# A two-block network on one core: bias tables made in steps, last down sums kept in SBUF, gate operands loaded a step earlier

## The chip, the cores and the metric

One core of one Trainium2 chip runs the whole program. The metric is device time in microseconds (us): 3697.61 is the median of three runs of the kernel before (3693.20, 3697.61 and 3698.63). All arithmetic is float32; a matrix product is made of three passes over operands split into a high part (fp32r) and a low rest.

## The reference

Two blocks run one after the other on 2048 positions of 1024 features. The change touches the feed-forward part of the first block, the two norms behind it and a table for the attention of the second.

```python
def first_block(x, ...):
    h = concatenate([meta, x])                    # 16 + 2048 positions
    ...                                           # state-space mixer, pooling mixer, two norms
    h = h + mixed @ w_out
    n2 = rmsnorm(h, norm2_g)
    ff = silu(n2 @ w_gate) * (n2 @ w_up)          # 1024 -> 2816
    h = h + ff @ w_down                           # 2816 -> 1024
    return rmsnorm(h, final_norm_g)[:, 16:]

def second_block(x, p, ...):
    h = layer_norm(x, ln_in_g, ln_in_b)
    ...                                           # w_in_2; band attention and gated linear attention
    bias = rel_table[:, rel_idx]                  # relative bias, rel_idx clipped to 257 entries a head
    ...
    h = layer_norm(r + gate * (p @ w_ple), ln_g, ln_b)
```

## The kernel before

Features lie on the 128 partitions and positions in the free dimension, so a tile is 128 features by 512 positions (256 KB), and there are eight such tiles (m, or k) by four blocks of positions (b). The program is traced line by line into one list. A planner then simulates that list with its own costs and writes out the order of every engine's queue: an instruction that is ready in the simulation may be put ahead of ones traced before it. On the chip each queue (PE, DVE, ACT, POOL, and SP, which issues all loads; ACT issues all stores) runs strictly in its written order and waits where an operand is late.

`phase_main` (L794) goes through these stages around the change. `mix_out` (L954) multiplies the mixed features by w_out, adds x, stores h1 and sums squares. `gu_half(half)` (L1073) makes the gate and up products for two blocks: 22 columns j, each of seven half-size products (a Strassen-like scheme with operands 1, 2, 6, 5, 7, 3, 4), 84 matmuls of 512 positions a column. Its right-hand operands, 56 tiles, come from `gu_in(half)` (L984): four steps k, each of which loads four h1 tiles, scales them and splits seven combinations. Its left-hand operands come from `gu_w(j)` (L1028), a generator of five steps: split of the gate weights; load of the up weights and a subtraction; s2 with the split tiles wth and wtl; wsh and wsl; the split of the up weights. `gu_prime` (L1067) starts it for column 0. `down(half)` (L1174) multiplies the hidden features (tile hin, loaded back from hid_d) by w_down for one block after the other (i = 0, 1), 22 steps of 24 matmuls, then adds h1, stores h3 and sums squares (sq) and g-weighted values (sz). `norm(b)` (L1227) is the final RMS norm and the input layer norm of block b: `total` (L780) sums over partitions with a ones-matmul, a first pass writes z back to h3 and sums its squares, a second pass writes h2. `proj_half(0, 0)` (L1345) is the first half of the w_in_2 product: 16 groups of 24 matmuls of 256 columns, then 16 groups of 24 of 512.

Background generators stand in a list, `bg`, and `bg_step` (L893) advances the first of them by one `yield`: `gu_in(0)` during mix_out, `gu_in(1)` during down(0), norm(0) and norm(1) during gu_half(1), norm(2) and norm(3) during proj_half(0, 0). `bias_table` (L1414) is called whole between gu_half(0) and down(0): for each of eight heads it loads 257 values a partition into a tile `e`, negates them, copies one of them 511 times and stores 768 values.

Tiles of one tag share a fixed number of places: `raw` has four, `nh`, `wru`, `hid`, `st2`, `sq` and `s` two, `ls` three, `wsh` and `wsl` one, `x` in the pool fp twenty. `slot` (L1147) gives out six places in a fixed turn, wru, wru, wsh, wsl, hid, hid, to hin (22 a block) and to the four h1 pairs of each block; the bias tile `e` has the tag wru too. A place is given in the order of the trace, and its next user waits for the last reader of the one before.

Of the kernel before, what the change touches and what calls it, by code (L numbers as in the profile page):

```python
# [6 lines left out]
F32 = mybir.dt.float32  # L7
# [3 lines left out]
ALU = mybir.AluOpType  # L11
# [3 lines left out]
KT = 8  # L15
# [12 lines left out]
NFF = 22  # L28
# [7 lines left out]
class Build:  # L36
# [757 lines left out]
    def phase_main(self):  # L794
# [4 lines left out]
        with ExitStack() as ctx:  # L799
# [11 lines left out]
            with tc.tile_pool(name="ffn", bufs=1) as self.fp:  # L811
                self.xr.append(self.fp)
                with tc.tile_pool(name="psf", bufs=8, space=PSUM) as self.ps:
                    self.ffn = True
                    self.w_next.append(self.get_w(0))
                    self.xm = {b: [None] * KT for b in range(4)}
                    for part in (1, 0):
                        ins = [self.mix_in(b, part) for b in (0, 1)]
                        self.bg = ins
                        self.run_bg()  # L820
                        if part:
                            start = self.mix_start()
                    self.bg = [self.mix_in(b, part) for b in (2, 3) for part in (1, 0)]
                    self.mix_out((0, 1), start)
                    self.run_bg()
                    self.bg = [self.gu_in(0)]
                    self.mix_out((2,), steps=(4,))
                    self.mix_out((3,), steps=(3,), last=True)
                    self.run_bg()
                    for half in range(2):  # L830
                        self.bg = [self.norm(0), self.norm(1)] if half else []
                        self.gu_half(half)
                        self.run_bg()
                        if half == 0:
                            self.bias_table()
                            self.bg = [self.gu_in(1)]
                        else:
                            self.bg = [self.proj_in_steps()]
                        self.down(half)
                        self.run_bg()  # L840
                    self.bg = [self.norm(2), self.norm(3)]
                    xs = self.xs1
                    self.proj_half(0, 0, xs)
                    self.run_bg()
                    self.ffn = False
                self.xr.pop()
# [137 lines left out]
    def gu_in(self, half):  # L984


        r = []
        for i in range(2):
            t = self.fp.tile([128, 512], F32, tag="ls", name="r2", bufs=3)
            self.load(t, self.r2_d[2 * half + i:2 * half + i + 1].to_broadcast([128, 512]))  # L990
            r.append(t)
        self.xg = {p: [] for p in (1, 2, 6, 5, 7, 3, 4)}
        g = self.vec["norm2_g"]
        for k in range(4):
            x = {p: self.xtile() for p in self.xg}
            four = []
            for kk, i in ((k, 0), (k, 1), (k + 4, 0), (k + 4, 1)):
                t0 = half * 1024 + i * 512
                f = self.tmp("raw", 4)
                self.load(f, self.h1_d[kk * 128:(kk + 1) * 128, t0:t0 + 512])  # L1000
                self.stt(f, f, g[:, kk:kk + 1], r[i], ALU.mult, ALU.mult)
                four.append(f)
            b11, b12, b21, b22 = four
            t1 = self.tmp("t", 2)
            self.tt(t1, b12, b11, ALU.subtract)
            self.halves(x[1], b11)
            self.halves(x[2], b21)
            self.tt(b11, b22, t1, ALU.subtract)
            self.halves(x[6], b11, self.pool)
            self.halves(x[5], t1)  # L1010
            self.tt(b12, b22, b12, ALU.subtract)
            self.halves(x[7], b12)
            self.halves(x[3], b22, self.pool)
            self.tt(b21, b21, b11, ALU.subtract)
            self.halves(x[4], b21)
            for p in x:
                self.xg[p].append(x[p])
            yield 1

    def gu_load(self, j, up):  # L1020
# [132 lines left out]
    def down_start(self, half):  # L1153

        self.order = []
        for b in (2 * half, 2 * half + 1):
            self.order += [(b, j, None) for j in range(NFF)] + [(b, None, q) for q in range(4)]
        self.got = []

    def fetch(self):  # L1160
        if self.order:
            b, j, q = self.order.pop(0)
            if q is None:
                x = self.slot([128, 2, 512], F32R, "hin")
                self.load(x.bitcast(F32), self.hid_d[b, j])
            else:
                x = self.slot([128, 2, 512], F32, "h1")
                self.load(x, self.pair(self.h1_d, b, q))
            self.got.append(x)
# [4 lines left out]
    def down(self, half):  # L1174


        gf = self.vec["final_norm_g"]
        self.fetch()
        self.stats = []
        for i in range(2):  # L1180
            b = 2 * half + i
            pss = []
            for j in range(NFF):
                x = self.got.pop(0)
                hi, lo = self.get_w()
                for m in range(KT):
                    if j == 0:
                        pss.append(self.ps.tile([128, 512], F32, tag="ps", name="dn", bufs=8))
                    self.mm3(pss[m], [hi[:, m]], [lo[:, m]], [x[:, 0]], [x[:, 1]], first=j == 0, last=j == NFF - 1)
                self.fetch()  # L1190
                if (j % 5 == 2) if half == 0 else i:
                    self.bg_step()
            if i and half == 0:
                self.gu_prime()
            if i:
                sq, sz = (self.fp.tile([128, 512], F32, tag="st2", name="st2", bufs=2) for _ in range(2))
            else:
                sq, sz = self.tmp("s", 2), self.tmp("s", 2)
            for q in range(4):
                x = self.got.pop(0)  # L1200
                for e in range(2):
                    m = 2 * q + e
                    self.stt(x[:, e], pss[m], 0.5, x[:, e], ALU.mult, ALU.add)
                    self.add_sq(sq, x[:, e], m == 0)
                    if m:
                        self.stt(sz, x[:, e], gf[:, m:m + 1], sz, ALU.mult, ALU.add)
                    else:
                        self.ts(sz, x[:, e], gf[:, 0:1], ALU.mult)
                self.store(self.pair(self.h3_d, b, q), x)
                self.fetch()  # L1210
            self.stats.append((sq, sz))
        if half == 0:
            for _ in self.gw_steps:
                pass
# [12 lines left out]
    def norm(self, b):  # L1227

        vec = self.vec
        gf = vec["final_norm_g"]  # L1230
        c = slice(b * 512, b * 512 + 512)
        sq, sz = self.stats[b % 2]

        def tiles(k):
            out = []
            for i in range(k, min(k + 2, KT)):
                t = self.fp.tile([128, 512], F32, tag="nh", name="nh", bufs=2)
                self.load(t, self.h3_d[i * 128:(i + 1) * 128, c])
                out.append((i, t))
            return out  # L1240

        mt = self.fp.tile([128, 512], F32, tag="ls", name="mt", bufs=3)
        self.ts(mt, self.total(sz), 1.0 / D, ALU.mult)
        r = self.rstd(self.tp, self.total(sq), 512, 1.0 / D, EPS, "ls", 3, self.fp)
        ts = tiles(0)
        yield 1
        sv = self.tmp("s", 2)
        for k in range(0, KT, 2):
            for i, z in ts:
                self.stt(z, z, gf[:, i:i + 1], mt, ALU.mult, ALU.subtract)  # L1250
                self.add_sq(sv, z, i == 0)
                self.store(self.h3_d[i * 128:(i + 1) * 128, c], z)
            ts = tiles(k + 2)
            yield 1
        ts = tiles(0)
# [5 lines left out]
        s = self.rstd(self.tp, sr, 512, 1.0 / D, LN_EPS, "ls", 3, self.fp)  # L1261
# [152 lines left out]
    def bias_table(self):  # L1414


        for h in range(8):
            e = self.fp.tile([128, KT, 128], F32, tag="wru", name="e", bufs=2).rearrange("p a b -> p (a b)")
            self.load(e[:, 511:768], self.a["rel_rev"][:, h])
            self.ts(e[:, 511:768], e[:, 511:768], -1.0, ALU.mult)  # L1420
            self.dve.tensor_copy(out=e[:, 0:511], in_=e[:, 511:512].to_broadcast([128, 511]))
            self.store(self.eb_d[:, h * 768:(h + 1) * 768], e[:, 0:768])

    def att_setup(self):
        p = self.ap_
# [496 lines left out]
```

## Time and profile before

| what | value |
|---|---|
| median of three runs | 3697.61 us |
| the profiled execution, its own time | 3690.3 us |
| its span, first to last instruction | 3688.4 us |
| busy share: PE, PEld, DVE, ACT, POOL | 90, 75, 56, 42, 43 % |
| HBM read, written | 417.43, 154.33 MB |

PE is TensorE's matmul queue and PEld its weight loads; PEclk is the TensorE clock granted, 1.00 being 2.4 GHz and 0.50 being 1.2 GHz. "[6.60 <-ACT sq L54]" behind an instruction says that its engine stood idle for 6.60 us before it and that an ACT instruction that wrote tile sq ended the idle time. SPq and ACTq are the instructions that issue DMAs. The program's places of the change are found by the tile names: mo is mix_out, pa, pb and pc are gu_half, dn is down, pv and pt are proj_half, st is `total`.

### The profile page before, as it was taken

What the parts mean: (1) busy time and instruction counts of PE and PEld (TensorE: products, weight loads), DVE (VectorE), ACT (ScalarE), POOL (GpSimd) and SP (SyncE); (2) the same over time, 40 slices, a digit from 0 to 9 for tenths busy, and PEclk for the clock granted to TensorE, in tenths of its full rate; (3) what the DMA queues carried; (4) which work ended last, traced back from release to release, by engine and by line L of the source; (5) the groups of instructions that cost most, each with busy time, mean ns of one, the idle gap of its engine ahead of it and who ended that gap; (6) DMA issues with size and microseconds to landing.
All of it is one profiled execution on the core that took longest, in us unless ns stands there. A gap on an engine that the chain in (4) does not pass through costs nothing. (4 is left out here: it accounts for less than half of the span.)

```text
span 3688.4 us, 45750 instructions
## 1 busy us (share of the span) xinstructions
PE 3327.0 (90%) x16138; PEld 2757.7 (75%) x16138; DVE 2075.1 (56%) x3365; ACT 1564.6 (42%) x2748; POOL 1569.6 (43%) x1146
## 2 busy tenths in 40 slices
PE   7897798799996998999999966999999999989887
PEld 7676576588885886777887865798888987767666
DVE  7776555666667106777632052234666446788783
ACT  5344533334333213444432232234655445666553
POOL 1265544454444445555445432322322225354443
PEclk9998899899998999999999988999999999989998
DMA  9643375333226664444376556565665565555351
GB/s 254 132 127 88 109 214 174 109 115 112 105 103 228 205 222 155 155 143 148 109 238 235 185 175 188 167 179 171 175 174 147 167 172 173 162 146 154 118 174 38
DMA packets 338204, 584.87 MB, mean 159 GB/s; under 512 B 85772, under 2 KB 171300, under 8 KB 337976
## 3 DMA queue, kind: packets, MB, share of 16 engines
q1 hardware_dynamic: 231552, 427.60, 39.4%
q10 hardware_dynamic: 106424, 154.36, 12.0%
q8 instruction: 127, 2.08, 0.2%
q14 instruction: 101, 0.83, 0.1%
HBM read 417.43 MB, written 154.33 MB: 155 GB/s over the span
## 5 line engine op out<-in xcount | busy, mean ns | idle before, releaser
L44 POOL TENSOR_TENSOR wl<-wr,wh 128x1024 fp32r<-128x1024 f32 (+1 forms) x235 | 583.2, 2484 | 580.5 <-ACT wh L54 518.9
L54 ACT ACTIVATE wh<-wr 128x1024 fp32r<-128x1024 f32 (+2 forms) x289 | 301.4, 1046 | 468.2 <-PE dn L164 267.4
L163 PE MATMUL pt<-xh,wh 128*128 128x512 f32 x896 | 361.7, 404 | 14.7 <-ACT wh L54 7.6
L165 PE MATMUL pt<-xh,wl 128*128 128x512 f32 x896 | 359.2, 402 | 3.5 <-POOL wl L44 2.7
L164 PE MATMUL pt<-xl,wh 128*128 128x512 f32 x896 | 359.3, 401 | 0.2 <-DVE xl L44 0.2
L163 PE MATMUL dn<-hin,wh 128*128 128x512 f32 x704 | 278.9, 396 | 34.4 <-DMA hin<-hid_d 33.4
L164 PE MATMUL dn<-hin,wh 128*128 128x512 f32 x704 | 278.1, 395 | 0.0
L48 POOL TENSOR_SCALAR P<-P,rsm 128x640 f32<-128x640 f32 (+4 forms) x128 | 102.8, 804 | 343.6 <-DVE rsm L1497 286.3
L51 DVE SCALAR_TENSOR_TENSOR h<-dn,h 128x512 f32<-128x512 f32 x32 | 19.8, 680 | 368.4 <-PE dn L165 368.4
L1083 PE MATMUL pa<-xh,wh 128*128 128x512 f32 x528 | 211.4, 400 | 12.2 <-ACT xh L54 4.5
L165 PE MATMUL dn<-hin,wl 128*128 128x512 f32 x704 | 222.1, 396 | 0.4 <-POOL wl L44 0.4
L1083 PE MATMUL pa<-xl,wh 128*128 128x512 f32 x528 | 210.0, 398 | 2.3 <-DVE xl L44 2.3
L163 PEld LDWEIGHTS pt<-xh,wh 128*128 128x128 f32 x896 | 171.3, 191 | 51.9 <-ACT wh L54 9.9
L44 POOL TENSOR_TENSOR wl<-wru,wh 128x1024 fp32r<-128x1024 f32 x44 | 108.4, 2463 | 237.0 <-ACT wh L54 236.8
L1083 PE MATMUL pa<-xh,wl 128*128 128x512 f32 x528 | 206.8, 398 | 0.7 <-POOL wl L44 0.7
L165 PEld LDWEIGHTS pt<-xh,wl 128*128 128x128 f32 x896 | 170.4, 190 | 41.7 <-POOL wl L44 5.4
L164 PEld LDWEIGHTS pt<-xl,wh 128*128 128x128 f32 x896 | 171.0, 191 | 35.5 <-DVE xl L44 0.7
L44 POOL TENSOR_TENSOR hid<-raw,hid 128x512 fp32r<-128x512 f32 x88 | 127.0, 1453 | 164.9 <-issue 87.7
L163 PEld LDWEIGHTS dn<-hin,wh 128*128 128x128 f32 x704 | 132.9, 189 | 67.9 <-issue 33.9
L165 PEld LDWEIGHTS dn<-hin,wl 128*128 128x128 f32 x704 | 132.8, 189 | 31.8 <-POOL wl L44 0.8
L164 PEld LDWEIGHTS dn<-hin,wh 128*128 128x128 f32 x704 | 133.0, 189 | 30.8
L1360 PE MATMUL pv<-wh,xh 128*128 128x256 f32 (+1 forms) x512 | 148.0, 291 | 6.1 <-ACT wh L54 2.6
(463 smaller groups left out, 9280.6 us busy)
## 6 DMA issues: line engine op xcount, KB each, us to landing
hid_d<-hid ACTq DMA_DIRECT2D x88, 512.0 KB, 3.4
wr<-in_w_down SPq DMA_DIRECT2D x88, 512.0 KB, 3.5
hin<-hid_d SPq DMA_DIRECT2D x88, 512.0 KB, 4.3
wr<-in_w_out SPq DMA_DIRECT2D x56, 512.0 KB, 4.6
raw<-h_d SPq DMA_DIRECT2D x96, 256.0 KB, 4.0
wr<-in_w_in SPq DMA_DIRECT2D x44, 512.0 KB, 3.9
wru<-in_w_up SPq DMA_DIRECT2D x44, 512.0 KB, 3.6
wr<-in_w_gate SPq DMA_DIRECT2D x44, 512.0 KB, 3.4
```

The costliest lines, as they stand in the source:

```text
L44: return (eng or self.dve).tensor_tensor(out=o, in0=x, in1=y, op=op)
L48: (eng or self.dve).tensor_scalar(out=o, in0=x, scalar1=s1, scalar2=s2, op0=op0, **kw)
L51: return self.dve.scalar_tensor_tensor(out=o, in0=x, scalar=s, in1=y, op0=op0, op1=op1)
L54: return self.act.activation(out=o, in_=x, func=func, **kw)
L163: self.pe.matmul(ps, lhsT=hi[k], rhs=xh[k], start=(first and k == 0), stop=False)
L164: self.pe.matmul(ps, lhsT=hi[k], rhs=xl[k], start=False, stop=False)
L165: self.pe.matmul(ps, lhsT=lo[k], rhs=xh[k], start=False, stop=(last and k == n - 1))
L1083: self.pe.matmul(ps, lhsT=l_[:, k], rhs=x[k][r_], start=(first and k == n == 0), stop=(k == 3 and n == 2), skip_group_check=True)
L1360: self.pe.matmul(pt, lhsT=xh, rhs=whi[:, k % 4], start=(k == 0), stop=False)
```

## The change

`bias_table` becomes a generator that yields after each head, uses two tiles of the tag nh in place of one of the tag wru, stores in two parts, and runs as background of gu_half(0). `gu_in` takes its loads into tiles of the tags nh and s, issues those of step k + 1 at the end of step k, keeps r in st2 and t1 in ls, and has six yields in place of four; mix_out calls it at steps 4 and 6 of block 2 and 1 and 4 of block 3, down(0) at j = 1, 5, ... of its first block. `down(1)` writes its sums into tiles of its own (tag x of fp, eight a block) which `norm(2)` and `norm(3)` read and overwrite; the stores to h3 and the loads from it remain for norm(0) and norm(1) alone. norm(0) and norm(2) yield three times before they begin. At the end of down(0), `gu_w(0)` is advanced by two steps more before the sums, and the second block's h1 pairs skip the two wru places.

```diff
                     self.bg = [self.gu_in(0)]
-                    self.mix_out((2,), steps=(4,))
-                    self.mix_out((3,), steps=(3,), last=True)
+                    self.mix_out((2,), steps=(4, 6))
+                    self.mix_out((3,), steps=(1, 4), last=True)
                     self.run_bg()
                     for half in range(2):
-                        self.bg = [self.norm(0), self.norm(1)] if half else []
+                        self.bg = [self.norm(0), self.norm(1)] if half else [self.bias_table()]
                         self.gu_half(half)
                         self.run_bg()
                         if half == 0:
-                            self.bias_table()
                             self.bg = [self.gu_in(1)]
...
+        def fetch(k):
+            out = []
+            for n, (kk, i) in enumerate(((k, 0), (k, 1), (k + 4, 0), (k + 4, 1))):
+                t0 = half * 1024 + i * 512
+                f = self.tmp("s", 2) if n % 2 else self.fp.tile([128, 512], F32, tag="nh", name="nh", bufs=2)
+                self.load(f, self.h1_d[kk * 128:(kk + 1) * 128, t0:t0 + 512])
+                out.append((f, kk, i))
+            return out
+
+        four = fetch(0)
+        yield 1
         for k in range(4):
+            for f, kk, i in four:
+                self.stt(f, f, g[:, kk:kk + 1], r[i], ALU.mult, ALU.mult)
...
+            self.tt(t1, b12, b11, ALU.subtract)
+            self.tt(b12, b22, b12, ALU.subtract)
+            if k == 2:
+                yield 1
             x = {p: self.xtile() for p in self.xg}
...
+            if k < 3:
+                four = fetch(k + 1)
             yield 1
...
         for b in (2 * half, 2 * half + 1):
-            self.order += [(b, j, None) for j in range(NFF)] + [(b, None, q) for q in range(4)]
+            self.order += [(b, j, None) for j in range(NFF)]
+            if b == 1:
+                self.order.append(None)
+            self.order += [(b, None, q) for q in range(4)]
...
     def fetch(self):
+        if self.order and self.order[0] is None:
+            self.order.pop(0)
+            self.slot_n += 2
...
-                if (j % 5 == 2) if half == 0 else i:
+                if (j % 4 == 1 and not i) if half == 0 else i:
                     self.bg_step()
             if i and half == 0:
                 self.gu_prime()
+                next(self.gw_steps)
+                next(self.gw_steps)
...
-                    self.stt(x[:, e], pss[m], 0.5, x[:, e], ALU.mult, ALU.add)
-                    self.add_sq(sq, x[:, e], m == 0)
+                    o = x[:, e]
+                    if half:
+                        o = self.fp.tile([128, 512], F32, tag="x", name="h3", bufs=20)
+                        kept.append(o)
+                    self.stt(o, pss[m], 0.5, x[:, e], ALU.mult, ALU.add)
+                    self.add_sq(sq, o, m == 0)
...
-                self.store(self.pair(self.h3_d, b, q), x)
+                if not half:
+                    self.store(self.pair(self.h3_d, b, q), x)
...
+                if kept:
+                    out.append((i, kept[i]))
+                    continue
                 t = self.fp.tile([128, 512], F32, tag="nh", name="nh", bufs=2)
                 self.load(t, self.h3_d[i * 128:(i + 1) * 128, c])
...
+        for _ in range(3 if b % 2 == 0 else 0):
+            yield 1
         mt = self.fp.tile([128, 512], F32, tag="ls", name="mt", bufs=3)
...
-                self.store(self.h3_d[i * 128:(i + 1) * 128, c], z)
+                if not kept:
+                    self.store(self.h3_d[i * 128:(i + 1) * 128, c], z)
...
         for h in range(8):
-            e = self.fp.tile([128, KT, 128], F32, tag="wru", name="e", bufs=2).rearrange("p a b -> p (a b)")
-            self.load(e[:, 511:768], self.a["rel_rev"][:, h])
-            self.ts(e[:, 511:768], e[:, 511:768], -1.0, ALU.mult)
-            self.dve.tensor_copy(out=e[:, 0:511], in_=e[:, 511:512].to_broadcast([128, 511]))
-            self.store(self.eb_d[:, h * 768:(h + 1) * 768], e[:, 0:768])
+            e, f = (self.fp.tile([128, 512], F32, tag="nh", name="e", bufs=2) for _ in range(2))
+            self.load(e[:, 0:257], self.a["rel_rev"][:, h])
+            self.ts(e[:, 0:257], e[:, 0:257], -1.0, ALU.mult)
+            self.dve.tensor_copy(out=f, in_=e[:, 0:1].to_broadcast([128, 512]))
+            c = self.eb_d[:, h * 768:(h + 1) * 768]
+            self.store(c[:, 0:512], f)
+            self.store(c[:, 512:768], e[:, 1:257])
+            yield 1
```

## Rows read from the trace of the kernel before

**Rows 1.** PE by stretch: from:to, length, busy (matmuls), granted clock, DMA share, GB/s.

```profile
573.38:708.10 134.72, 101.67 (x372) 0.85 0.46 148
708.10:1128.20 420.10, 420.06 (x1814) 1.00 0.30 109
1128.20:1200.00 71.80, 40.42 (x160) 0.76 0.73 244
1405.00:1480.00 75.00, 56.72 (x231) 0.89 0.45 153
1480.00:1874.40 394.40, 386.97 (x1643) 0.99 0.41 141
2119.40:2328.50 209.10, 147.50 (x781) 0.85 0.55 177
2141.20:2156.00 14.80, 14.80 (x126) 1.00 0.57 182
```

**Rows 2.** PE's waits, whole run: who waited for whom, us, times, longest.

```profile
PE st L790 <- ACT sq L54: 59.4, 6, 31.5
PE dn L163 <- DMA hin<-hid_d: 33.4, 5, 30.7
...
PE pa L1083 <- ACT wth L54: 14.7, 1, 14.7
```

**Rows 3.** PE's waits between 573.38 and 708.10 us, the stretch around gu_in(0).

```profile
PE st L790 <- ACT sq L54: 9.9, 2, 6.6
PE pc L1083 <- ACT wsh L54: 6.6, 1, 6.6
PE pa L1083 <- ACT xh L54: 4.5, 1, 4.5
```

**Rows 4.** DVE's waits in the same stretch, the longest.

```profile
DVE raw L51 <- DMA raw<-h_d: 21.6, 8, 4.2
```

**Rows 5.** SP's queue at the beginning of down(0), order of time: start, length.

```profile
1124.95 4.66 SPq L57 DMA_DIRECT2D raw<-h_d  x3
...
1172.62 5.86 SPq L57 DMA_DIRECT2D e<-in_rel_rev  x2
...
1186.09 12.41 SPq L57 DMA_DIRECT2D hin<-hid_d  x2
```

**Rows 6.** The bias tile e: ns min/median/max, first and last start; then landing times.

```profile
L48 DVE TENSOR_SCALAR e<-e x8: 283/288/2495, 1138.8 to 1180.9; 128x257 f32<-128x257 f32 x8
L1421 DVE COPY e<-e x8: 414/427/2442, 1139.1 to 1182.9; 128x511 f32<-128x511 f32 x8
...
DMA to landing us min/median/max: 2.3/5.0/7.3
```

**Rows 7.** SP's queue between down(0) and gu_half(1), order of time.

```profile
1409.29 3.69 SPq L57 DMA_DIRECT2D wru<-in_w_up  x2
```

**Rows 8.** DVE between down(0) and gu_half(1), order of time, first and last sum.

```profile
1402.52 2.48 DVE L51 SCALAR_TENSOR_TENSOR h<-dn,h 128x512 f32<-128x512 f32 x4 [104.88 <-PE dn L165]
...
1419.19 2.82 DVE L51 SCALAR_TENSOR_TENSOR st<-h,v_final_norm_g,st 128x512 f32<-128x512 f32 x1
```

**Rows 9.** PE's waits between 2119.4 and 2328.8 us, proj_half(0, 0).

```profile
PE st L790 <- ACT sq L54: 49.1, 3, 31.5
PE pt L163 <- ACT wh L54: 5.7, 1, 5.7
PE pv L1361 <- POOL wl L44: 2.9, 1, 2.9
```

**Rows 10.** DVE's waits between 2135 and 2253 us, the longest.

```profile
DVE nh L51 <- DMA nh<-h_d: 43.1, 16, 6.5
```

**Rows 11.** DVE by line, 2119 to 2253 us: count, busy us, mean ns, idle before.

```profile
L51 DVE SCALAR_TENSOR_TENSOR nh<-nh,v_final_norm_g,mt 128x512 f32<-128x512 f32 x16 | 13.0, 819 | 31.3 <-DMA nh<-h_d 30.7 <-ACT ev L54 0.6
L51 DVE SCALAR_TENSOR_TENSOR st<-h,v_final_norm_g,st 128x512 f32<-128x512 f32 x7 | 10.6, 1520 | 0.2
```

**Rows 12.** POOL by line, 2135 to 2253 us, the squares of the norms summed.

```profile
L44 POOL TENSOR_TENSOR s<-s,sq 128x512 f32<-128x512 f32 x14 | 18.7, 1333 | 50.6 <-ACT sq L54 50.4
```

More of the change, by code (lines that the diff above doesn't have):

```diff
@@ L988, in gu_in @@
         for i in range(2):
-            t = self.fp.tile([128, 512], F32, tag="ls", name="r2", bufs=3)
+            t = self.fp.tile([128, 512], F32, tag="st2", name="r2", bufs=2)
             self.load(t, self.r2_d[2 * half + i:2 * half + i + 1].to_broadcast([128, 512]))
@@ L993, in gu_in @@
         g = self.vec["norm2_g"]
-        for k in range(4):
-            x = {p: self.xtile() for p in self.xg}
[L996 to L1005, printed above, removed]
+        def fetch(k):
[8 more added lines that the diff above has]
+        yield 1
+        for k in range(4):
+            for f, kk, i in four:
+                self.stt(f, f, g[:, kk:kk + 1], r[i], ALU.mult, ALU.mult)
+            b11, b12, b21, b22 = (f[0] for f in four)
+            t1 = self.fp.tile([128, 512], F32, tag="ls", name="t1", bufs=3)
+            self.tt(t1, b12, b11, ALU.subtract)
+            self.tt(b12, b22, b12, ALU.subtract)
+            if k == 2:
+                yield 1
+            x = {p: self.xtile() for p in self.xg}
             self.halves(x[1], b11)
@@ L1010, in gu_in @@
             self.halves(x[5], t1)
-            self.tt(b12, b22, b12, ALU.subtract)
             self.halves(x[7], b12)
@@ L1194, in down @@
                 self.gu_prime()
+                next(self.gw_steps)
+                next(self.gw_steps)
+            kept = []
             if i:
@@ L1202, in down @@
                     m = 2 * q + e
-                    self.stt(x[:, e], pss[m], 0.5, x[:, e], ALU.mult, ALU.add)
-                    self.add_sq(sq, x[:, e], m == 0)
+                    o = x[:, e]
[4 more added lines that the diff above has]
+                    self.add_sq(sq, o, m == 0)
                     if m:
-                        self.stt(sz, x[:, e], gf[:, m:m + 1], sz, ALU.mult, ALU.add)
+                        self.stt(sz, o, gf[:, m:m + 1], sz, ALU.mult, ALU.add)
                     else:
-                        self.ts(sz, x[:, e], gf[:, 0:1], ALU.mult)
-                self.store(self.pair(self.h3_d, b, q), x)
+                        self.ts(sz, o, gf[:, 0:1], ALU.mult)
+                if not half:
+                    self.store(self.pair(self.h3_d, b, q), x)
                 self.fetch()
-            self.stats.append((sq, sz))
+            self.stats.append((sq, sz, kept))
         if half == 0:
@@ L1231, in norm @@
         c = slice(b * 512, b * 512 + 512)
-        sq, sz = self.stats[b % 2]
+        sq, sz, kept = self.stats[b % 2]
         def tiles(k):
```

## The prediction

> **What bounds the kernel now.** I read the busy shares first: PE is busy 90% of the span, no other engine over 56%. So I went on to PE by stretch [rows 1], to see where the missing tenth lies. The gate product of the first half runs 1814 matmuls in 420.06 of 420.10 us at clock 1.00: that is the price of a matmul of 512 positions when nothing is late, 0.2316 us. Those of 256 columns cost 14.80/126 = 0.1175 us. With these, each stretch that the diff touches has a floor and an excess:
>
> - A, gu_in(0) around the end of mix_out: 372 x 0.2316 = 86.2, took 134.7, excess 48.6 us, of it 33.1 idle; the rest is matmuls at a clock below 1.00 after the stalls (0.85 in the mean), so an idle us costs 48.6/33.1 = 1.47 us here.
> - B, the beginning of down(0): 160 x 0.2316 = 37.1, took 71.8, excess 34.7, 31.4 idle.
> - C, the beginning of gu_half(1): 231 x 0.2316 = 53.5, took 75.0, excess 21.5, 18.3 idle.
> - D, proj_half(0, 0): 384 of 256 columns 45.1, the other 397 at 0.2316 91.9, together 137.0; took 209.1, excess 72.1, 61.6 idle.
>
> In all 176.9 us that edits of this kind can reach. PE's waits over the run say who holds them [rows 2]: totals of the norms waiting for a split sum 59.4, down waiting for hin 33.4, a gate product waiting for wth 14.7. They are three of the largest, and each lies in one of the four stretches.
>
> **The change part by part.** Durations are of the profiled execution, 3690.3 us (its span 3688.4); the median of the runs is 7.3 us above it, and I take the sum of gains from the median.
>
> *B, the bias table.* Down(0) stands still for one hin, 30.7 us. SP's order shows why: the last two loads of e go out at 1172.62, and the hin that PE needs only at 1186.09 [rows 5]. The tag decides it: e and hin share the two wru places, eight e were traced ahead of the seventh hin, so that hin waits for four rounds of load, two DVE operations and a store. With e in nh the six places of `slot` belong to hin alone. What stays are the sixteen 256 KB loads of gu_in(1), which have this place in both versions. Bounds: all 34.7 gone, or 15 if these loads alone keep SP's queue late by half. I take 30: each hin is then asked for up to six steps of 24 x 0.2316 = 5.6 us ahead.
>
> *The bias heads' new place.* Two yields in odd columns and one in even ones put the eight heads into the first six columns of gu_half(0), 84 x 0.2316 = 19.5 us each. They add 8 x (0.29 + 0.43) = 5.8 us of DVE, up to 8 x (2.50 + 2.44) = 39.5 where POOL is in the way, and eight loads, sixteen stores on ACT's queue; a load or a store takes 2.3 to 7.3 us to land [rows 6]. The cover is good (DMA share 0.30, PE never idle [rows 1]) but the queues are strict: an early-placed negation waits for its load and holds the DVE work behind it, a store waiting for the copy holds ACT. The least is nothing. The most I charge is the slower rival's price below. I take 2 us lost.
>
> *A, gu_in(0).* PE waits there 9.9 us for totals, 6.6 for wsh, 4.5 for xh [rows 3], and DVE waits eight times, 21.6 us, for h1 tiles [rows 4]: its scaling of an h1 tile stands in front of mix_out's evacuation and of the weight splits, and only four raw places, shared with mix_out's own x tiles, carry the loads. Afterwards four loads of a step go out together, a step ahead, from places of their own: one wait per k in place of two, so half of 21.6. Not covered: step 3's loads can only start when step 2's tiles are read, and those need the x places that block 3 of mix_out frees at its end, so one round (median 5.0 us to land, as for e in [rows 6]) and some 5 us of DVE stay behind the last mo, against 63 gate matmuls (14.6 us) that k = 0 to 2 already allow. I count the longer of the two total waits (6.6) and two thirds of wsh and xh (7.4) as gone: 14 us idle, times 1.47 = 21. Ends: nothing, if the planner writes the scaling as close behind the loads as now; 34 if only the first total (3.3), weight splits and their clock remain.
>
> *C, the gate operands.* The up weights for column 0 are asked for at 1409.29 [rows 7], after PE has left down, since their wru place held an h1 pair. s2 and wth then queue on DVE behind the sums of down, which fill it from 1402.5 to 1422.0 [rows 8], and PE waits 14.7 us [rows 2]. Afterwards the place is free from j = 17 on, four steps or 22 us earlier, and s2 and wth are traced ahead of the sums, in a stretch where DVE had been idle for 104.9 us [rows 8]. wsh and wsl come next: their places now hold the first two h1 pairs, and wsl's subtraction stays behind the sums, not before 1422. PE then has products 1, 2, 6 and two thirds of 5, 44 matmuls or 10.2 us from 1405.0: it waits for about 7 us instead of 14.7. Gain 8, and 1 for norm(0) coming three steps later: 9. Ends: 0 (POOL's splits are as late as wth was) and 15.
>
> *D, the sums kept.* DVE waits sixteen times, 43.1 us, for nh tiles coming back from h3 [rows 10], and PE's totals behind it 49.1 us, another 5.7 for a weight split that ACT could not reach behind the norm's operations [rows 9]. The change takes away 32 loads of 256 KB and the stores of h3 and z, 16 MB; the arithmetic stays. What is late next is arithmetic: a first pass is 8 scalings on DVE (0.82 us), 8 squares on ACT and 7 additions on POOL (1.33) [rows 11, 12], paced by POOL at 10 to 11 us. From norm(2)'s first total to its second lie six background steps, of 24 x 0.1175 = 2.8 us, 17 us, and norm(3)'s lie partly among the 512-column groups (5.6 us each), so both are covered. Three groups (8.5 us) now stand ahead of norm(2)'s first total. Left: 2.9 for a w_av split on POOL, about 5 around the first totals, while DVE and POOL work off down's sums, 2 at the end, 2 of clock: 12 of 72. Gain 60. Ends: 24 (ports, below) and 69.
>
> Here the Trainium skill speaks against the change: SBUF — State Buffer, section Who interferes with whom, says that a DVE instruction with two SBUF inputs and a GpSimd instruction that reads SBUF take one shared port in turn, each for its whole length. The trace bears it out: the same kind of operation takes 0.82 us in a first pass that waits for DMA and 1.52 beside POOL's back-to-back additions [rows 11]. By that rule a first pass without DMA pauses takes 8 x (0.82 + 1.33) = 17 us in place of 11.
>
> *Sum.* 30 - 2 + 21 + 9 + 60 = 118 us; 3697.6 - 118 = 3580. Everything after 2330 has the same instructions; but the planner orders anew, for which I allow 10 us either way.
>
> **The rivals.**
> - *Ports.* First passes take 8 x (0.82 + 1.33) = 17 to 18 us, and if the planner writes the totals directly behind each other, PE stands through two of them, 36 us: D gives 72 - 12 - 36 = 24, the sum is 82, 3616 us. For: [rows 11]. Against: six steps of other matmuls are traced between.
> - *The lead does nothing.* The planner already hoists whatever is ready, so moved yields and earlier `next` calls change nothing where a place or a queue is the limit: A gives 5, C 2, the sum is 95, 3603 us. For: the first loads of gu_in(1), traced at j = 2 of down(0), go out at 1124.95 already [rows 5], before down's own stretch begins. Against: the tags change too, not the order alone.
> - *All of it.* A 34, B 34, C 15, D 69, nothing lost: 152, 3546 us. Against: POOL's splits and the first totals stay.
> - *Slower: the bias heads break the gate stage.* nh has two places, one head fills both, and SP is strict: a load of e waiting for the store before it holds the gate and up weights queued behind it. Price: 8 heads x (one landing 5.0 + load 5.0 + 0.7 DVE) = 86 us, times 1.47 for the clock 126 us; more than the 118 gained, so 3706 us. It decides from 80 us idle, 10 us a head; below it the change still gains. Against: the weights are loaded a column of 19.5 us ahead, and one or two heads fall into a column.
>
> **How the numbers follow.** Forecast 50%, ports 18%, the lead does nothing 16%, all of it 12%, slower 4%. The forecast alone runs from 3560 to 3602 (A and D 10 us each way, B and C 5, the new order 10). The range goes to the ports' price plus the planner's 10 above, and to the full gain less 6 below: 3540 to 3628. All cases but the last lie below 3690, which is 0.2% under the median, about what a measurement of this kernel can tell from no change: faster 0.95, same 0.01, slower 0.04.
>
> **What would show it.** B: no wait of down for hin over 3 us, e loads between 700 and 830 us. D: no h3 loads after down(1), PE's waits for totals in proj_half(0, 0) under 10 us in all, its stretch near 149 us. A: DVE's waits for h1 tiles halved, the stretch to the steady gate columns near 114 us. C: the wait moved from wth to wsl or wl and halved. The gate stage still at clock 1.00 and within 2 us of 420. Wrong would be a wait for totals of over 20 us in D, PE idle in the first six gate columns, or a new wait after 2330.

## The result, and the profile after

The changed kernel takes 3607.5 us, the median of four runs (3604.7 to 3610.5); the kernel before took 3695.6 beside it. The ratio is 0.9761, 95% interval [0.9744, 0.9778]: 88 us faster, where 118 were forecast. That is inside the stated range, but 5.5 us above the 3560 to 3602 of the forecast alone. Run again beside the last three versions it gave 3605.0. The profiled executions differ by 85.7 us of span (3688.4 and 3602.7), and the points where PE changes stage divide that up (the first stretch begins where PE stops for the first total, at 573):

| stretch on PE | before | after | gain | forecast |
|---|---|---|---|---|
| last blocks of mix_out (gu_in(0) beside them) | 98.5 | 106.9 | -8.4 | |
| gu_half(0) | 456.5 | 449.9 | 6.6 | 19 with the row above (A 21, heads -2) |
| down(0) (B) | 276.7 | 256.2 | 20.5 | 30 |
| gu_half(1) (C) | 469.6 | 456.0 | 13.6 | 9 |
| down(1) | 244.9 | 243.8 | 1.1 | 0 |
| proj_half(0, 0) to the first score matmul (D) | 220.7 | 170.5 | 50.2 | 60 |
| everything behind | 1348.4 | 1346.1 | 2.3 | 0 |

PE by stretch, cut at these points, before and then after; the columns are those of [rows 1]:

```profile
573.38:671.90 98.52, 82.13 (x319) 0.90 0.53 169
671.90:1128.40 456.50, 439.81 (x1870) 0.98 0.30 108
1128.40:1405.05 276.65, 243.99 (x1040) 0.94 0.65 217
1405.05:1874.60 469.55, 443.84 (x1873) 0.97 0.42 143
2119.45:2340.10 220.65, 158.97 (x825) 0.85 0.56 179
```

```profile
573.20:680.10 106.90, 84.00 (x320) 0.87 0.54 168
680.10:1130.00 449.90, 438.66 (x1870) 0.99 0.34 120
1130.00:1386.20 256.20, 246.36 (x1038) 0.98 0.64 212
1386.20:1842.20 456.00, 442.29 (x1879) 0.99 0.42 145
2086.00:2256.50 170.50, 156.67 (x832) 0.95 0.45 149
```

PE's waits over the whole run after, the two longest in total (who waited for whom, us, times, longest):

```profile
PE z L753 <- ACT ge L54: 29.0, 9, 9.2
PE st L790 <- ACT sq L54: 19.7, 5, 8.2
```

Against [rows 2], down's wait for hin (33.4) and the gate product's for wth (14.7) are gone, and the totals' wait has fallen from 59.4 to 19.7. Of these 19.7, 13.5 lie in the first stretch, where 9.9 lay before [rows 3]:

```profile
PE st L790 <- ACT sq L54: 13.5, 2, 8.2
PE mo L165 <- DVE wl L44: 6.0, 2, 5.5
PE pa L1092 <- DVE wtl L44: 3.8, 1, 3.8
PE mo L165 <- POOL wl L44: 2.6, 1, 2.6
PE pa L1092 <- POOL wl L44: 2.1, 1, 2.1
```

This is the view (573.2 to 700 us) where the term with the largest miss, A, failed. In place of the waits of the first gate products, 6.6 for wsh and 4.5 for xh [rows 3], there are 3.8 for wtl and 2.1 for wl; but the totals' waits grew (6.6 to 8.2 and 3.3 to 5.3) and a weight split of mix_out became late. Next, DVE in that stretch (from:to, length, busy, clock, DMA share, GB/s); before, it was busy for 63.1 of the same 100 us:

```profile
600.00:700.00 100.00, 77.44 (x78) 0.86 0.50 153
```

What stands in front on DVE's queue can be read off in order of time:

```profile
614.81 0.75 DVE L51 SCALAR_TENSOR_TENSOR s<-s,v_norm_g,r 128x512 f32<-128x512 f32 x1 [2.00 <-DMA s<-h_d]
615.48 1.22 DVE L44 TENSOR_TENSOR wl<-wr,wh 128x1024 fp32r<-128x1024 f32 x1
...
635.77 2.65 DVE L51 SCALAR_TENSOR_TENSOR s<-s,v_norm_g,r 128x512 f32<-128x512 f32 x2 [1.66 <-DMA s<-h_d]
...
641.41 0.68 DVE L44 TENSOR_TENSOR t<-mo,raw 128x512 f32<-128x512 f32 x1
```

PE ran out of work at 611.3 and waited 5.5 us for the weight split of 615.48, whose other half was ready at 610.4; a scaling of gu_in that still waits for its load stands ahead of it. PE ended the last sum of block 2 at 635.5; its evacuation came at 641.41, behind seven operations of gu_in, and the total waited 8.2 us.

The bias heads run at the beginning of gu_half(0), but eight in 48 us, some three to a column, where one or two were expected. The tile e after (ns min/median/max, first and last start), and ACT's waits for it between 690 and 760 us:

```profile
L57 SPq DMA_DIRECT2D e<-in_rel_rev x8: 327/328/333, 694.4 to 738.7; - x8
L48 DVE TENSOR_SCALAR e<-e x8: 281/298/1378, 699.3 to 741.2; 128x257 f32<-128x257 f32 x8
...
  DMA e<-in_rel_rev: 10.3, 6
```

```profile
ACT wsh L54 <- DVE e L48: 8.1, 1, 8.1
ACT wsh L54 <- DVE e L1451: 7.0, 1, 7.0
ACT raw L54 <- DVE e L1451: 5.4, 1, 5.4
```

SP's queue, which issues the loads, waited in turn for the heads' stores (688 to 760 us):

```profile
SPq L57 <- DMA eb_d<-e: 35.7, 9, 5.9
```

One head's store on ACT waits for DVE's copy, the copy for DVE's negation, the negation for a load (10.3 us of DVE in six waits) that SP often could issue only after an earlier store had landed. As I read it, what stands behind the store on ACT, an evacuation or a weight split, is what PE lacks next. (A wait "for e" of the split wsh is a wait of the queue: the store, which is not shown as busy, stands ahead of it.)

In proj_half(0, 0) PE's waits came down from [rows 9] to these, 13.8 us in all:

```profile
PE st L790 <- ACT sq L54: 5.1, 2, 3.8
PE pt L163 <- DVE ev L51: 2.2, 1, 2.2
PE st L791 <- DVE sl L44: 2.0, 2, 1.7
PE pv L1390 <- ACT wh L54: 1.9, 1, 1.9
PE pt L165 <- POOL wl L44: 1.7, 1, 1.7
PE pv L1390 <- DVE ev L44: 0.9, 1, 0.9
```

### The profile page after: what moved, and what is told of

The parts are those of the page before. It is cut to its first block, busy times and chain, and to the rows that moved or that the text cites. A ratio compares the mean times of both kernels' runs of the same rounds, so it can differ in the third digit from the quotient of the medians.

```text
span 3602.7 us, 45654 instructions
## 1 busy us (share of the span) xinstructions
PE 3326.9 (92%) x16138; PEld 2761.8 (77%) x16138; DVE 2092.3 (58%) x3365; ACT 1565.5 (43%) x2750; POOL 1569.8 (44%) x1146
## 4 chain that ended last, share of the span: by engine, by line
PE 36%; DVE 7%; DMA 5%; ACT 3%; issue 2%; POOL 1%; SPq 0%; ACTq 0%; DVEq 0%; POOLq 0%
PE pt L165 4%; PE pt L163 4%; PE pt L164 4%; PE pa L1092 3%; PE dn L163 2%; PE dn L164 2%; PE dn L165 2%; PE pv L1562 2%; PE s L1520 1%; PE pv L1391 1%; PE pv L1392 1%; PE pc L1092 1%; PE pv L1390 1%; PE tp L1546 1%; DMA raw<-mix_d 1%
## 5 line engine op out<-in xcount | busy, mean ns | idle before, releaser
L1525 DVE CUSTOM_DVE_ANT_0 P<-s,bias 128x640 f32<-128x640 f32 (+4 forms) x128 | 94.5, 738 | 108.5 <-PE s L1520 59.9
```

The source lines that it names most:

```text
L1525: self.dve.tensor_tensor_reduce(out=v3(P[:, 0:w]), in0=sp[:, 0:np_, 0:n], in1=v3(bias[:, 640 - w:640]), scale=1.0, scalar=3e38, op0=ALU.ad ...
```

## Experiments

All stretches below are cut as in the table. In these runs the last one, with the same matmuls (6859 to 6867 records), took between 1334 and 1352 us without any order by kernel, and so the stretches tell more than the totals.

### 1. The bias table back in the wru places

```diff
-            e, f = (self.fp.tile([128, 512], F32, tag="nh", name="e", bufs=2) for _ in range(2))
+            e = self.fp.tile([128, KT, 128], F32, tag="wru", name="e", bufs=2)...
...
-                        self.bg = [...] if half else [self.bias_table()]
+                        self.bg = [...] if half else []
...
+                            self.bias_table()
                             self.bg = [self.gu_in(1)]
```

> The changed kernel with one part undone: the bias table is again one call between gu_half(0) and down(0), with its tile e in the tag wru. Theory (places): the eight tiles stand again between the sixth and the seventh hin, PE waits for hin 20 to 30 us and down(0) takes some 22 us longer, while the gate stage, rid of the heads, gives back 2 to 8; about 3622 us, 3617 to 3630. Rival (the queue): down(0) was held by gu_in(1)'s loads in SP's queue, which now have places of their own; then this kernel stays within 5 us of the changed one, 3602 to 3612, and no wait for hin exceeds 10 us.

3623.8 us, ratio 0.9816 [0.9797, 0.9834], 16 more than the change, as the theory has it. gu_half(0) and down(0), and the wait that came back:

```profile
678.30:1119.70 441.40, 434.79 (x1870) 0.99 0.32 112
1119.70:1400.50 280.80, 244.53 (x1038) 0.95 0.63 208
```

```profile
PE dn L163 <- DMA hin<-hid_d: 26.9, 3, 25.1
```

Down(0) pays 24.6 us for the shared places (280.8 against 256.2); gu_half(0) without heads is 8.5 us shorter (441.4 against 449.9). So the step is worth 16 net, and the heads cost four times the 2 us that I charged.

### 2. gu_in as before: loads in their own step

```diff
-                f = self.tmp("s", 2) if n % 2 else self.fp.tile(..., tag="nh", ...)
+                    f = self.tmp("raw", 4)
...
-                    self.mix_out((2,), steps=(4, 6))
-                    self.mix_out((3,), steps=(1, 4), last=True)
+                    self.mix_out((2,), steps=(4,))
+                    self.mix_out((3,), steps=(3,), last=True)
...
-                if (j % 4 == 1 and not i) if half == 0 else i:
+                if (j % 5 == 2) if half == 0 else i:
```

> The changed kernel with gu_in as it was (places raw, t and ls, no loads a step ahead, four yields at the old steps). Theory (the work only moved): in the changed kernel gu_in's DVE operations come earlier and stand in front of mix_out's evacuations and weight splits instead of the first gate column, so undoing it changes little: 3600 to 3614 us, and mix_out's last matmul falls back by some 8 us while the first gate columns lose the same. Rival (the gain is there but the bias heads eat it): undoing gu_in costs the 21 us that were forecast for it, 3622 to 3634 us.

3605.1 us, 0.9759 [0.9739, 0.9779]: no difference in the total. As a whole the new gu_in gains nothing in this pair of runs: what it gains in one place is given back in another. From its own profile, mix_out's end, gu_half(0) and down(0), each against the row of after above:

```profile
580.80:682.00 101.20, 85.59 (x319) 0.88 0.53 166
682.00:1136.20 454.20, 438.70 (x1869) 0.98 0.30 108
1136.20:1388.60 252.40, 243.85 (x1039) 0.99 0.66 223
```

The old gu_in is 5.7 us better beside mix_out and 3.8 better in down(0). But the heads stood elsewhere in this run, and only run 11 with runs 1, 5 and 10 separates the two (below).

### 3. The down sums stored again

```diff
-                    if half:
+                    if False:
                         o = self.fp.tile([128, 512], F32, tag="x", name="h3", bufs=20)
...
-                if not half:
+                if True:
                     self.store(self.pair(self.h3_d, b, q), x)
```

> The changed kernel with down(1) again writing its sums to h3 and norm(2) and norm(3) loading them back twice; the three yields before norm(2) stay. Theory (DMA paced the norms): proj_half(0, 0) takes some 50 us longer, 3650 to 3662 us, with DVE waiting for nh again for over 30 us. Rival (half of the gain came from norm(2) beginning three steps later): it takes 20 to 35 us longer, 3628 to 3643 us.

3647.7 us, 0.9878 [0.9860, 0.9896], 40 more than the change: between the two ranges, nearer to the theory's. DVE waits again for nh, 45.9 us in fifteen times. The stretch of proj_half(0, 0), and PE's and DVE's waits that came back:

```profile
2088.30:2297.90 209.60, 159.84 (x824) 0.86 0.60 188
```

```profile
PE st L790 <- ACT sq L54: 43.8, 3, 31.1
```

```profile
DVE nh L51 <- DMA nh<-h_d: 45.9, 15, 6.2
```

209.6 against 170.5: 39 us of D's 50 belong to the kept sums. The other 11 (220.7 to 209.6) come with the rest of the change: the first total waits 3.9 us in this run, as in the change, where it waited 8.5 before, and the 5.7 for wh [rows 9] does not occur. The first of these is what three yields ahead of norm(2) should do, but the yields weren't tried alone.

### 4. Gate operands as late as before

```diff
                 self.gu_prime()
-                next(self.gw_steps)
-                next(self.gw_steps)
...
-            if b == 1:
-                self.order.append(None)
```

> The changed kernel without the two extra steps of gu_w(0) and without the two places skipped at the end of down(0). Theory (place and order): PE waits again some 15 us for wth at the first column of gu_half(1), 3617 to 3625 us. Rival (the gain at this place came from norm(0) beginning three steps later, which stays): 3605 to 3612 us.

3612.2 us, 0.9784 [0.9762, 0.9805]: the time lies between the two ranges, at the rival's end, and decides nothing. The wait does, and it is the theory's: all 14.7 us [rows 2] are back in gu_half(1). First this run, then the change:

```profile
PE pa L1092 <- ACT wth L54: 14.7, 1, 14.7
```

```profile
PE pc L1092 <- DVE wsl L44: 3.7, 1, 3.7
```

The change waits for wsl, as predicted. The stage takes 472.1 us against 455.5 to 462.8, 459.8 in the mean, in the nine profiles with the early operands and no heads in this stage: C is worth 12 against the mean, 9 to 17 against the ends. I forecast 9.

### 5. The bias table traced in down(1)

```diff
-                        self.bg = [...] if half else [self.bias_table()]
+                        self.bg = [...] if half else []
...
-                            self.bg = [self.proj_in_steps()]
+                            self.bg = [self.bias_table(), self.proj_in_steps()]
...
-                if (j % 4 == 1 and not i) if half == 0 else i:
+                if (j % 4 == 1 and not i) if half == 0 else (i or j % 2 == 0):
```

> The bias table is built in down(1)'s background, ahead of proj_in_steps, instead of gu_half(0)'s. Theory: the bias heads in gu_half(0) cost 8 to 10 us of TensorE idle time (e1_bias_old's gate stage was that much shorter without them), because their DVE operations stand in front of splits that TensorE waits for; down(1) has little other background, so there they cost 0 to 4: stage of gu_half(0) 440 to 442 us instead of 450, down(1) 244 to 248, time 3598 to 3603. Rival: any place costs the same 8 to 10, because a head's transposes and gathers need the same engines everywhere: down(1) 252 to 254, time within 3 us of 3607.

3604.6 us, 0.9763 [0.9745, 0.9781], the rival's time by another way than it said (a head has no transposes or gathers, and down(1) paid nothing). gu_half(0) fell to 443.7 as the theory has it and down(1) stayed at 242.6, but gu_half(1) rose to 464.8. The tile e shows why:

```profile
L48 DVE TENSOR_SCALAR e<-e x8: 297/298/1549, 1705.9 to 1747.0; 128x257 f32<-128x257 f32 x8
```

Traced behind gu_half(1), which ends at 1841, the heads were put a hundred us forward into it by the planner, and the stage is 5 us above the mean of run 4's nine. So this run is no test of down(1) as a place. The last line of the edit also lets down(1)'s first block advance its background, which proj_in_steps did not do before; down(1) shows no cost of it.

### 6 and 8. Additions of squares from POOL to DVE

```diff
-                    self.add_sq(sq, o, m == 0)                               # run 6, in down
+                    self.add_sq(sq, o, m == 0, self.dve if i else None)
...
-                self.add_sq(sv, z, i == 0)                                   # run 8, in norm
+                self.add_sq(sv, z, i == 0, self.dve if kept else None)
```

> The second block's additions of squares behind the down sums go to DVE instead of POOL, so that POOL is free for the weight splits at the start of the stages behind both down stages. Theory: the stages' first matmuls wait for the weight split (3.7 us at gu_half(1), 1.7 at proj_half(0,0)), and DVE has room in down: 2 to 5 us less, 3602 to 3606. Rival: DVE ends each down sum itself, and the additions lengthen the chain behind the last matmul: 3 to 8 us more, 3611 to 3616.

> In the norms that read the kept sums (norm 2 and 3), DVE adds the squares instead of POOL. The first scaling on DVE took 1.06 and 1.58 us each beside POOL's additions, against 0.82 before. Theory of the shared port: alone, DVE's scaling falls back to 0.75 to 0.85 us, but 16 additions of 1.1 to 1.4 us each come to DVE, which is on the path in this stage: stretch of proj_half(0,0) 160 to 175 us instead of 158.6, time 3608 to 3622. Rival: the additions are hidden, since TensorE waits little in this stretch after the first 40 us, and the faster scaling counts: stretch 150 to 157, time 3600 to 3606.

3597.7 us, 0.9742 [0.9722, 0.9761], and 3599.3, 0.9748 [0.9725, 0.9771]. The stretch of proj_half(0, 0) is 168.4 and 164.1 instead of 170.5. Run 6 is faster than its theory, but not by it: in gu_half(1) a wait of 4.1 us for wtl took the place of the 3.7 for wsl (the stage took 462.8), and most of the 10 us lie in the last stretch (1336). Run 8 speaks on the port. DVE by line, 2085 to 2200 us (count, busy us, mean ns, idle before), first after, then run 8:

```profile
L51 DVE SCALAR_TENSOR_TENSOR h<-h,v_final_norm_g,mt 128x512 f32<-128x512 f32 x16 | 21.3, 1399 | 0.0
```

```profile
L51 DVE SCALAR_TENSOR_TENSOR h<-h,v_final_norm_g,mt 128x512 f32<-128x512 f32 x16 | 15.0, 1010 | 0.0
...
L44 DVE TENSOR_TENSOR s<-s,sq 128x512 f32<-128x512 f32 x14 | 11.6, 827 | 0.3
```

The scaling that took 819 ns with pauses for DMA [rows 11] took 1399 in the mean beside POOL's additions (1479 ns each there) and 1010 without them; an addition costs DVE 827 ns. These means mix two kinds of operation. Two pairs of POOL and DVE instructions in the kernel after (start, length) show the dear kind:

```profile
2106.96 1.41 POOL L44 TENSOR_TENSOR s<-s,sq 128x512 f32<-128x512 f32 x1 [5.13 <-ACT sq L54]
2107.12 1.79 DVE L51 SCALAR_TENSOR_TENSOR h<-h,v_final_norm_g,mt 128x512 f32<-128x512 f32 x1
...
2150.54 2.83 POOL L44 TENSOR_TENSOR wl<-wr,wh 128x1024 fp32r<-128x1024 f32 x1 [26.02 <-DMA vh_d<-ev]
2151.06 2.86 DVE L51 SCALAR_TENSOR_TENSOR h<-h,v_final_norm_g,mt 128x512 f32<-128x512 f32 x1
```

A scaling that begins while POOL is inside an instruction ends some 0.55 us after that instruction (2108.37 and 2108.91, 2153.37 and 2153.92); every other one takes 0.74 to 0.75 us. Of the sixteen after, eight are held up in this way, six by additions and two by weight splits; of run 8's sixteen two are, both by weight splits. So fourteen of the sixteen have the price that the theory gave; what failed in it is the path. The stretch shortened as the rival said: cut as in the expectation it is 152.1 us instead of 158.6, and PE idles 9.6 us in the whole stretch instead of 13.8. That the additions are hidden because the evacuations behind the scalings come sooner is how I read it.

### 7. Without gu_in(1)

```diff
-                            self.bg = [self.gu_in(1)]
+                            self.bg = []
```

> Leaves out part of the computation: gu_in(1), the normalised gate operands of the second half; gu_half(1) multiplies the first half's again, with the same number of matmuls. It shows what preparing them costs beside down(0). Theory: down(0) is still 12 to 16 us longer than down(1) (256 against 244) because of these operations' DVE and ACT work and their loads in the weights' queue: down(0) 240 to 244, gu_half(1) within 4 us of 456, time 3590 to 3597. Rival: down(0)'s excess is the change of stage itself (the first weights of w_down behind the gate stage): down(0) 252 to 256, time 3603 to 3608.

3589.9 us, 0.9724 [0.9707, 0.9742]. Down(0):

```profile
1126.10:1370.10 244.00, 240.74 (x1039) 1.00 0.64 214
```

12.2 us less than after, and level with down(1) (243.0 in this run): all that down(0) still loses is the preparation of the gate operands, 12 loads in the queue of the weights and the arithmetic. (The planner had put the first four of gu_in(1)'s 16 loads, and their scalings, into gu_half(0), from 683.7 to 751.3 us. gu_half(1) took 460.9, a microsecond outside the theory's bound and inside the scatter of that stage in run 4.)

### 9, 10 and 11. Combinations, beside the change once more

Run 9 is 6 and 8 together, run 10 adds the edit of run 5, run 11 that of run 2.

> The changed kernel once more, as the measure for the three beside it on the same chip. Expected: 3604 to 3611, its earlier runs, against 3686 to 3698 before; its stretches within 5 us of those of its first profile.

> Both moves of additions of squares from POOL to DVE: those of the second block's down sums, and those of norms 2 and 3. If the two add, as the stretches of their own runs say (164.1 and 168.4 instead of 170.5 us to the first score, the rest unchanged): 9 us less in that stretch and 3597 to 3601. Rival: both free the same POOL and the second brings nothing: stretch 163 to 166, time 3600 to 3605 and no better than either alone.

> As the run with both moves of additions, and the bias table in down(1)'s background. Theory: the bias heads cost gu_half(0) 6 to 9 us and down(1) nothing, so 6 to 9 less than that run: 3590 to 3595; the longer gate stage of the second half in the run with the moved bias table alone (465 instead of 456) was scatter of that stage. Rival: that 9 us belongs to the move, and this run is within 2 us of the one with both moves of additions, its gu_half(1) 463 to 467.

> As the run before it, with gu_in as it was: loads in the step that uses them, into the old places. Theory: the loads a step ahead gain some 6 us up to the end of gu_half(0) and give back 4 in down(0), so this run is 1 to 4 us slower: 3592 to 3598. Rival: without bias heads in the background of gu_half(0), the stage waits for the operands alone, and the earlier loads count in full: 10 to 20 us slower, 3602 to 3612.

The change again: 3605.0, 0.9769 [0.9745, 0.9792], with single runs from 3593.6 to 3619.7. Run 9: 3598.0, 0.9747 [0.9729, 0.9764]; the two moves add (161.8 us instead of 170.5). Run 10: 3603.1, 0.9755 [0.9740, 0.9771]; its theory fails, and the rival is right on the cause but too low in size: 5 us above run 9, not 2, and gu_half(1) at 470.4, with the heads in it again (1709 to 1750 us). Run 11: 3595.6, 0.9738 [0.9722, 0.9753], the lowest median, though its interval overlaps that of the change, so that no version is shown to beat it. PE in its first four stretches:

```profile
572.10:671.30 99.20, 82.49 (x320) 0.90 0.54 172
671.30:1128.00 456.70, 440.15 (x1869) 0.97 0.30 107
1128.00:1379.70 251.70, 243.79 (x1038) 0.99 0.66 224
1379.70:1852.40 472.70, 450.20 (x1879) 0.97 0.43 148
```

Both expectations on run 11 had it slower than run 10; up to gu_half(0) it is, by 8 us (555.9 against 547.6), but down(0) gives 5 back, the norms 3, and the last stretch was 9 shorter, which is scatter.

## Why the prediction was right or wrong

The direction, the places and the two largest terms, D and B, in their order were right; the sum was 30 us too large, and A, forecast third, came last of the four gains. Together the first two stretches tell A and the bias heads apart:

| mix_out's end and gu_half(0), us | heads elsewhere | heads in gu_half(0) |
|---|---|---|
| gu_in as before | 555.0 (before), 555.4 (run 2), 555.9 (run 11) | not run |
| gu_in a step ahead | 548.0, 548.3, 547.6 (runs 1, 5, 10) | 556.8 and 556.5 (after, again), 553.5 to 556.5 in six more |

**A, forecast 21, measured 7 to 8, less 4 in down(0).** The step that failed is "I count the longer of the two total waits (6.6) and two thirds of wsh and xh (7.4) as gone". The second half held: the gate's first waits fell from 13.4 us (6.6, 4.5 and 2.3 for xl) to 5.9, by 7.5. So did the tell: DVE's waits for gu_in(0)'s h1 tiles fell from 21.6 [rows 4] to 8.1 (three of 7.1 in all and one of 1.0). But I treated DVE's idle time as the cost and its removal as the gain. DVE filled it with the scalings and combinations of gu_in, which now stand ahead of mix_out's evacuations and weight splits: the total's wait grew from 6.6 to 8.2 and that for the split at 616.7 from 0.8 to 5.5. The first total's grew too, from 3.3 to 5.3, but there DVE waits 4.5 us for a store of h1 and no operation of gu_in is ahead of it; it goes with the new gu_in in every run, and why stays open. In the eleven profiles with the new gu_in these three waits are 7.4 to 9.1, 4.7 to 5.5 and 5.1 to 5.7, in the three with the old one 4.3 to 6.8, 0.8 to 1.1 and 2.4 to 3.3, and mix_out's end took 6 us longer in the mean (104.6 to 106.9 against 98.5 to 101.2). From 573.2 to 700 PE has run 366 matmuls, where 372 in 114 us were to be seen. In down(0) the same generator costs 4 us more than the old one (253.3 to 256.7 in nine profiles against 251.7 and 252.4); which of its changes does that was not tried.

**The bias heads, forecast -2, measured about -8.5.** "The cover is good" failed. The two strict queues that I named as the danger were real: the heads cost 8.5 us in gu_half(0) by run 1, 5 to 9 by the table, and gu_half(1) took 464.8, 470.4 and 472.7 when the planner put them there (runs 5, 10 and 11), 5 to 13 above the 459.8 without. In run 2 the planner put them at 478 to 548, and the stretch behind began at 580.8 instead of 568 to 575. It is about 1 us a head, a tenth of the price at which the slower rival decides. The gate stage was not "within 2 us of 420 at clock 1.00": PE idles 5.4 of the 130 us from 700 on, where it idled for 1.3 before and not at all in run 1. Over the whole of gu_half(0), 4.6 of the 8.5 us are idle time and 3.9 are longer matmuls.

**B, forecast 30, measured 24.6 by run 1, 20.5 in the profile.** The hin wait is gone and the mechanism stands. The mis-sized part is what stays: I left 4.7 us for gu_in(1)'s loads, and run 7 puts the whole of gu_in(1) at 12.2. Of these, 4 are A's. With the old gu_in, down(0) is 24.3 and 25.0 shorter than before (runs 2 and 11), which agrees with run 1.

**C, forecast 9, measured 13.6 in the profile, 9 to 17 by run 4.** The wait went from wth (14.7) to wsl (3.7) as worked out; I had left 7. The size is no surer than 9 to 17, as the stage scatters.

**D, forecast 60, measured 50.** I left 12 us of excess, 10 of them idle and 2 of clock; it came to 21.6: 13.8 us idle and, at a clock of 0.95, 7.8 us of longer matmuls (144.8 busy against the floor of 137.0; the stretch is 158.6 where 149 were to be seen). The clock is the term that I mis-sized most. Nor did the first passes take 10 to 11 us, paced by POOL: from the first scaling to the last addition the trace after has 14.5 (2104.5 to 2119.0) and 21.2 (2149.1 to 2170.3), the second with two weight splits of POOL among the additions. That is the ports rival's mechanism, on either side of the 17 estimated from the Trainium skill's rule (SBUF — State Buffer, section Who interferes with whom), that the two engines take the port in turn. Single operations in the trace agree with it: eight of the sixteen scalings wait out a POOL instruction (experiment 8). The rival's price, PE standing through both passes, did not come, since three steps stand ahead of the total and other matmuls between the totals, whose waits are 7.1 us in all. Run 8 takes 6 us of the 10 away.

**The sum.** 24.6 - 8.5 + 3.5 + 13.6 + 50.2 + 1.1 + 2.3 = 86.8 (B, the heads, A less its 4, C, D, down(1), the rest), against 85.7 of the spans. Of the rivals, "the lead does nothing" came nearest in time (3603), for its sign of A: a lead that the planner fills with other work is worth little; but on C it was wrong, since run 4 brings the whole wait back. That its time is 4 us off is in part luck: its C is 12 too low, and its B and D, taken from the forecast, are 15 too high.

## What to carry to other kernels

An engine's idle time in front of a late load is a gain only if nothing that it does instead stands in front of the critical chain: before counting a wait as gone, list what comes earlier on that queue and who is then second. Small background work whose load, arithmetic and store sit on three strict queues cost about a microsecond an item in the places where the planner put it (gu_half(0), gu_half(1), and by run 2's late start mix_out), so moving it gained nothing here; fewer items were not tried. Data kept on chip between two stages was the surest term here: 39 us for sixteen tiles that were stored twice and loaded back twice.

## What was not expected of the hardware

Eight DVE scalings of 128x512 float32 took 5.4 us in run 8 and 8.5 and 12.8 in the kernel after. What POOL did when each one began accounts for its length. All fourteen traces together have 448 of them. The 288 that begin while POOL runs nothing take 0.74 to 0.75 us, also where a POOL instruction begins during them. The other 160 begin while POOL is inside an addition or a weight split; all but one end 0.54 to 0.59 us after that instruction, which makes them up to 2.9 us long (the one began 0.02 us before POOL's end and took 0.75). A scaling has two inputs in SBUF; mix_out's evacuation, with one in PSUM and one in SBUF, took 0.67 to 0.76 us in all 64 cases before and after, 18 of them begun inside a POOL instruction.

The same matmuls behind the first score took 1334 to 1352 us in the thirteen profiles of the change and its variants, at clocks of 0.96 to 0.97; what moves them stays open, and it is as large as most edits tried here.
